# Seven-product groups in a decoder trunk: four products add up in one PSUM bank, and the last is put off into the next group

## The chip, the cores and the metric

The kernel runs on one core of a Trainium2 chip. A core has five engines with instruction queues of their own: TensorE (PE in the profile; its weight loads are listed apart as PEld), VectorE (DVE), ScalarE (ACT), GpSimd (POOL) and SyncE (SP, which here issues most of the weight transfers). Matmul results land in PSUM, eight banks of 128 partitions by 512 fp32 numbers; operands lie in SBUF. Each engine works through its queue in order and waits on semaphores where it needs another's result.

The metric is the time of one execution on the device in microseconds, as a median of several runs; lower is better.

## The reference

A two-layer decoder trunk on 512 tokens of width 1024, in float32: layer 0 mixes tokens by gated linear attention (GLA), layer 1 by stick-breaking attention (SB), and each layer is wrapped by two half-step feed-forward blocks (FFN), so there are four FFNs:

```python
x = x + 0.5 * swiglu(rmsnorm(x, ffn1_norm[i]), ffn1_w_gate[i], ffn1_w_up[i], ffn1_w_down[i])
h = rmsnorm(x, mix_norm[i])
y = gla_mixer(h, ...) if i % 2 == 0 else sb_mixer(h, ...)
x = x + y
x = x + 0.5 * swiglu(rmsnorm(x, ffn2_norm[i]), ffn2_w_gate[i], ffn2_w_up[i], ffn2_w_down[i])
# swiglu(h, g, u, d) = (silu(h @ g) * (h @ u)) @ d, with 1024 x 2816, 1024 x 2816 and 2816 x 1024 weights
```

A final rmsnorm ends it. The change lies in the four FFNs alone.

## The kernel before, in words

Activations are kept transposed: eight tiles `xs[k]` of 128 features by 512 tokens. Every fp32 product is made of three matmuls of rounded parts: an operand is cut into a high part (a cast on ACT) and a low part (a subtraction on DVE), and high·high, low·high and high·low are added up in PSUM (`mm3`; in the seven-product groups the loop in `prod`, L540 to L547). The cuts of the weights are lines 135 (ACT) and 136 (DVE), those of the activations lines 631 and 632.

**Feed.** The work of all phases that eats weights is one list of entries, `feed.q`. Starting an entry cuts the weights of the next entries and issues the transfers of the ones behind (`Feed.start`), then runs the entry's body, which issues its matmuls and evacuations.

**An FFN** works through eleven chunks of 256 columns of the gate and up weights, gathered in the groups of `GROUPS`, (0,2), (2,4), (4,6), (6,8), (8,9), (9,11). After a group, the matching rows of the down weights are multiplied with its hidden tiles `hs` in `down` entries, which are interleaved with the chunks of the next group. A `down` of a four-tile group takes 24 matmuls of 512 columns in two PSUM tiles; one of the two-tile group (8,9) 24 in four PSUM tiles. The last group's `down` entries stand at the end of the FFN (in the last FFN `back_tok` instead, behind transposes in `to_tokens`).

**Seven-product groups.** A dense chunk (1024 x 256 weights, 512 tokens) is cut into 2 x 2 x 2 blocks, eight products of 512 x 128 weights by 256 tokens. For the gate of chunks 3 to 10 and the up of chunks 2 to 10, `seven` replaces them by seven products and some additions (a Strassen-Winograd scheme). That makes 17 such groups in each FFN, 68 in all. Each product is 12 matmuls of 256 columns (four blocks of the contraction, three each). Two feed entries make a group: `body_1` with products 1 to 4 and `body_2` with 5 to 7. Before the change:

- product 1 goes to bank `w` and is copied out to `u2` (ACT, L580); product 2 goes to `z` and DVE adds it to `u2` (L556);
- product 3 goes to `q` and is copied to `c5` (ACT, L587); product 4 adds to product 1 in `w`, which is then the first half of the left result tile `o0` (`left`, L560 or L562);
- product 5 goes to the second half of the bank of `z` (called `y`); DVE adds `u2` to it (`u3`, L556), and then `c5` (L600), which is the second half of `o1`;
- product 6 adds to product 3 in `q`, DVE adds `u2` (L556), and `rest` finishes `o0` (L566 for a gate, L569 for an up);
- product 7 goes to the second half of the bank of `w`, DVE adds `u3` (L556), and `rest` finishes `o1`.

For a gate group `left` and `rest` are a Silu on ACT, and the tiles go to `self.gates`. For an up group they multiply with a gate tile on DVE, and `close` cuts the product into `hh` and `hl` and appends it to `hs`.

**Order.** Outside a few stretches marked as scheduled by hand, a planner in the framework lays out each engine's queue. It runs the program through a model of the engines' times and issues, among what is ready in that model, the instruction that stands first in the program. A tile whose slot is still held makes its instructions not ready. It also puts in every semaphore wait. Two accesses of one PSUM bank by different engines are kept apart by a wait even where they touch different columns.

**Banks.** `psum(name)` without a tag deals banks in the fixed round `order = "aazzztto"` over four pools of 2, 3, 2 and 1 banks. A seven-product group takes three turns, a `feat` one, a `down` two or four.

Of the kernel before, what the change touches and what calls it, by code (L numbers as in the profile page):

```python
# [19 lines left out]
P = 128  # L20
# [12 lines left out]
def decoder(ctx: ExitStack, tc: tile.TileContext, a: dict, out: bass.AP):  # L33
# [257 lines left out]

                feed.q.append(Entry([u], body))

    def down(w, r0, nf, hs, part, nxt):

        nd = KD // nf
        src = w[r0 : r0 + nf * P, part * nd * P : (part + 1) * nd * P]
        ch = Chunk(src.rearrange("(f p) c -> p f c", p=P), nf, nd * P)
        ch.few = True

        def body(W):
            (wh, wl), = W
            for m in range(nd):
                ps = psum("ps_d")
                s = slice(m * P, (m + 1) * P)
                for f in range(nf):
                    mm3(ps, wh[:, f, s], wl[:, f, s], hs[f][0], hs[f][1], f == 0, f == nf - 1)
                k = part * nd + m
                x = like(xs[k], 4)
                nc.vector.scalar_tensor_tensor(  # L310
                    out=x, in0=back_by(ps, 4), scalar=0.5, in1=x, op0=ALU.mult, op1=ALU.add
                )
                if nxt is not None:
                    nxt(k)
                yield

        feed.q.append(Entry([(ch, lambda t: t, nf, nd * P)], body))
# [135 lines left out]
    class FFN:  # L453
# [10 lines left out]
        def __init__(self, wg, wu, wd, gi, nxt, first=False, last=False):  # L464
            self.gi, self.normed, self.first = gi, False, first
            self.evac_g_, self.evac_u_ = self.evac_g, lambda ps: self.evac_u(ps, 0)
            if first:
                self.NORMED = 8
            self.defer, self.gates = [], []
            self.lead = []  # L470
            self.hs = [[] for _ in self.GROUPS]
            base, downs = len(feed.q), []
            self.base = base
            self.sums_by = 10**6
            for group, (c0, c1) in enumerate(self.GROUPS):
                slots, put = 2 * (c1 - c0), 0
                for i in range(slots):
                    c, f = c0 + i // 2, i % 2
                    if f == 0:
                        g, u = Chunk(cols(wg, c * 256, 256), KD, 256), Chunk(cols(wu, c * 256, 256), KD, 256)  # L480
                    d = self.defer if i == 0 and c == 0 else None
                    f_ = f
                    if first and c == 0:

                        g, u = (Chunk(cols(w, f * P, P), KD, P) for w in (wg, wu))
                        self.lead += [g, u]
                        f_ = 0
                    if c >= self.SEVEN:
                        if f == 0:
                            self.seven(g)  # L490
                    elif c not in self.SEVEN_UP:
                        feat(g, f_, self.evac_g, defer=self.defer if first and i == 1 else d, o=quads, m=four)
                    elif f == 0:
                        feat(g, 0, self.evac_g, o=quads, m=four), feat(g, 1, self.evac_g, o=quads, m=four)
                    if c not in self.SEVEN_UP:
                        feat(u, f_, lambda ps, h=group: self.evac_u(ps, h), defer=d, o=quads, m=four)
                    elif f == 1:
                        while c < self.SEVEN and put < len(downs) // 2:
                            down(*downs[put])
                            put += 1  # L500
                        self.sums_by = min(self.sums_by, len(feed.q) - base)
                        self.seven(u, group)

                    while c >= self.SEVEN and put < len(downs) * (i + 1) // slots:
                        down(*downs[put])
                        put += 1
                for x in downs[put:]:
                    down(*x)
                n = 2 * (c1 - c0)
                end = group + 1 == len(self.GROUPS)  # L510
                downs = [(wd, c0 * 256, n, self.hs[group], part, nxt if end else None) for part in range(n)]
            self.count = len(feed.q) - base
            if last:
                back_tok(wd, c0 * 256, n, self.hs[group], nxt)
            else:
                for x in downs:
                    down(*x)
            self.total = len(feed.q) - base

        def seven(self, ch, group=None):  # L520
# [31 lines left out]
            def part(name):  # L552
                return self.tp.tile([P, H], F32, tag="c", bufs=2, name=name)
# [10 lines left out]
            def rest(o, c):  # L564
# [4 lines left out]
                nc.vector.tensor_tensor(out=o[:, c:T], in0=o[:, c:T], in1=self.gates.pop(0)[:, c:T], op=ALU.mult)  # L569
                self.close(o, group)  # L570

            def body_1(W):
                ax, s = W

                v["w"], v["z"], v["q"] = psum("ps_w"), psum("ps_z"), psum("ps_q")
                w, z, q = (v[n][:, 0:H] for n in "wzq")
                v["o"] = self.tp.tile([P, T], F32, tag="t", name="o0")
                prod(w, ax, 0, half(0, 0))
                v["u2"] = part("u2")
                nc.scalar.copy(v["u2"], w)  # L580
                yield
                prod(z, s, 4, lambda j: self.t_half(1, j))
                add(v["u2"], z, v["u2"])
                yield
                prod(q, s, 0, lambda j: self.t_half(0, j))
                v["c5"] = part("c5")
                nc.scalar.copy(v["c5"], q)  # L587
                yield
                prod(w, ax, 4, half(4, 0), first=False)
                left(v["o"], w)  # L590
                yield

            def body_2(W):
                s, a22 = W
                q, y = v["q"][:, 0:H], v["z"][:, H:T]
                o0, o1 = v["o"], self.tp.tile([P, T], F32, tag="t", name="o1")
                prod(y, s, 0, lambda j: self.t_half(2, j))
                u3 = o1[:, 0:H]
                add(u3, y, v["u2"])
                nc.vector.tensor_tensor(out=o1[:, H:T], in0=u3, in1=v["c5"], op=ALU.add)  # L600
                yield
                prod(q, s, 4, half(4, 1), first=False)
                add(o0[:, H:T], q, v["u2"])
                rest(o0, H)
                yield
                o = v["w"][:, H:T]
                prod(o, a22, 0, lambda j: self.t_half(3, j))
                add(o1[:, 0:H], o, u3)
                rest(o1, 0)
                yield  # L610


            feed.q.append(Entry([(ch, lambda t: t[:, :, 0:P], KD, P), (ch, sums_12, KD, P)], body_1))
            feed.q.append(Entry([(ch, sums_34, KD, P), (ch, lambda t: t[:, 4:8, P:], 4, P)], body_2))

        def t_half(self, i, j):

# [71 lines left out]
        def run(self, between=None):  # L689
            with tc.tile_pool(name="hp", bufs=8, reuse_waits="tile") as self.hp, tc.tile_pool(  # L690
                name="tp", bufs=5, reuse_waits="tile"
            ) as self.tp:
                st["few"] = self.hp
                new_norm()

                if self.first:
                    with tc.manual_schedule():
                        feed.entries(1)
                        stats_b(turned=True)
                        flush(self.defer)  # L700
                else:
                    two_halves(stats_a)
                    stats_b(turned=True)
                    flush(self.defer)
                done = feed.pos - self.base
                for job, n in ((self.normed_input, self.NORMED - done), (self.sums, self.sums_by - self.NORMED)):
                    todo = list(job())
                    for i in range(n):
                        for piece in todo[i * len(todo) // n : (i + 1) * len(todo) // n]:
                            piece()  # L710
                        feed.entries(1)
                    self.normed = True
                    st["h"], st["l"] = zip(*self.n)
                feed.entries(self.count - self.sums_by)
                if between is not None:
                    with tc.issue_after(st["silu"]):
                        nc.scalar.preload_act_table_set("sqrt_and_others")
                    feed.q[feed.pos].split()
                    between(self.tp)
                feed.entries(self.total - self.count)  # L720
# [844 lines left out]
```

## Time and profile before

| what | value |
|---|---|
| median of 3 runs | 1797.32 us (1796.83 to 1797.62) |
| the profiled execution | 1798.32 us |
| its span, first to last instruction | 1796.5 us |
| mean granted TensorE clock | 0.997 |
| PE busy | 1771.0 us, 12,502 matmuls |
| DVE busy | 1450.4 us |
| ACT busy | 906.9 us |
| GLA mixer, about | 345 to 600 us |
| SB mixer, about | 1220 to 1460 us |

A busy share counts the time from an instruction's start to its end. Matmuls overlap in the array, so the profile's mean of one matmul is longer than the distance from one start to the next. How densely PE works is read from starts: in the chain that ended last, a run of matmuls is given with its start, its length and its count.

### The profile page before, as it was taken

What the parts mean: (1) busy time and instruction counts of PE and PEld (TensorE: products, weight loads), DVE (VectorE), ACT (ScalarE), POOL (GpSimd) and SP (SyncE); (2) the same over time, 40 slices, a digit from 0 to 9 for tenths busy, and PEclk for the clock granted to TensorE, in tenths of its full rate; (3) what the DMA queues carried; (4) which work ended last, traced back from release to release, by engine and by line L of the source; (5) the groups of instructions that cost most, each with busy time, mean ns of one, the idle gap of its engine ahead of it and who ended that gap; (6) DMA issues with size and microseconds to landing.
All of it is one profiled execution on the core that took longest, in us unless ns stands there. A gap on an engine that the chain in (4) does not pass through costs nothing.

```text
span 1796.5 us, 30288 instructions
## 1 busy us (share of the span) xinstructions
PE 1771.0 (99%) x12502; PEld 1622.2 (90%) x12502; DVE 1450.4 (81%) x2371; ACT 906.9 (50%) x1428; POOL 9.6 (1%) x23
## 2 busy tenths in 40 slices
PE   9999999999999999999999999999999999999998
PEld 7899999888988899999989999998877888999997
DVE  7988887787868988878898888786777579888785
ACT  6544445455645444444554444454777544544444
POOL 0000000100000000000000000000000000000000
PEclk9999999999999999999999999999999999999999
DMA  6243333321222333333333333322222223333321
GB/s 212 71 133 114 106 118 103 96 72 57 87 71 94 117 106 106 106 113 100 107 111 101 106 106 118 106 83 83 59 71 71 71 94 118 106 106 111 125 83 71
DMA packets 177614, 179.19 MB, mean 100 GB/s; under 512 B 4098, under 2 KB 167988, under 8 KB 177476
## 3 DMA queue, kind: packets, MB, share of 16 engines
q1 hardware_dynamic: 176224, 175.13, 30.4%
q8 instruction: 98, 1.61, 0.4%
q0 software_dynamic: 576, 1.05, 0.2%
q10 hardware_dynamic: 676, 1.07, 0.2%
q14 instruction: 40, 0.33, 0.1%
HBM read 175.17 MB, written 2.10 MB: 99 GB/s over the span
## 4 chain that ended last, share of the span: by engine, by line
PE 84%; DVE 9%; ACT 3%; DMA 3%; issue 1%; SPq 0%; DVEq 0%; ACTq 0%
PE ps_d L64 24%; PE ps_w L545 15%; PE ps_f L64 13%; PE ps_z L545 10%; PE ps_q L545 10%; PE ps_t L64 4%; PE ps_b L64 4%; DVE wl L136 2%; DMA raw<-in_ffn_w_up_dram 2%; DVE l L1211 1%; PE ps_bt L64 1%; ACT wh L135 1%; PE ps_z L1167 1%; DVE r L1219 1%; DMA raw<-in_sb_w_in_dram 1%
## 5 line engine op out<-in xcount | busy, mean ns | idle before, releaser
L136 DVE TENSOR_TENSOR wl<-raw,wh 128x1024 fp32r<-128x1024 f32 x242 | 259.4, 1073 | 72.2 <-ACT wh L135 71.6
L135 ACT CAST wh<-raw 128x1024 fp32r<-128x1024 f32 (+1 forms) x242 | 223.9, 927 | 149.4 <-PE ps_f L64 53.1
L64 PE MATMUL ps_d<-hh,wh 128*128 128x512 f32 x672 | 254.9, 379 | 0.0
L64 PE MATMUL ps_d<-hh,wl 128*128 128x512 f32 x672 | 254.7, 379 | 0.0
L64 PE MATMUL ps_d<-hl,wh 128*128 128x512 f32 x672 | 254.7, 379 | 0.0
L135 ACT CAST wh<-s 128x1024 fp32r<-128x1024 f32 x136 | 142.2, 1046 | 117.0 <-PE ps_q L545 80.3
L136 DVE TENSOR_TENSOR wl<-s,wh 128x1024 fp32r<-128x1024 f32 x136 | 166.0, 1222 | 24.1 <-ACT wh L135 23.0
L64 PE MATMUL ps_f<-xh,wh 128*128 128x512 f32 x464 | 180.7, 390 | 0.3 <-DVE ol L1257 0.2
L64 PE MATMUL ps_f<-xh,wl 128*128 128x512 f32 x464 | 176.9, 381 | 0.5 <-DVE wl L1444 0.4
L64 PE MATMUL ps_f<-xl,wh 128*128 128x512 f32 x464 | 177.0, 381 | 0.0
L310 DVE SCALAR_TENSOR_TENSOR x<-ps_d,x 128x512 f32<-128x512 f32 x184 | 125.2, 689 | 60.9 <-PE ps_d L64 60.7
L545 PE MATMUL ps_z<-th,wh 128*128 128x256 f32 x544 | 150.1, 276 | 0.2 <-DVE u L556 0.2
L545 PE MATMUL ps_w<-nh,wl 128*128 128x256 f32 x544 | 149.6, 275 | 0.0
L545 PE MATMUL ps_w<-nl,wh 128*128 128x256 f32 x544 | 149.6, 275 | 0.0
L545 PE MATMUL ps_z<-th,wl 128*128 128x256 f32 x544 | 149.6, 275 | 0.0
L545 PE MATMUL ps_z<-tl,wh 128*128 128x256 f32 x544 | 149.6, 275 | 0.0
L545 PE MATMUL ps_w<-nh,wh 128*128 128x256 f32 x544 | 149.5, 275 | 0.0
L135 ACT CAST wh<-rawd 128x1024 fp32r<-128x1024 f32 x84 | 88.0, 1048 | 121.5 <-PE ps_d L64 103.2
L64 PEld LDWEIGHTS ps_d<-hl,wh 128*128 128x128 f32 x672 | 127.0, 189 | 18.0
L64 PEld LDWEIGHTS ps_d<-hh,wl 128*128 128x128 f32 x672 | 127.2, 189 | 16.5
L64 PEld LDWEIGHTS ps_d<-hh,wh 128*128 128x128 f32 x672 | 127.2, 189 | 16.5
L136 DVE TENSOR_TENSOR wl<-rawd,wh 128x1024 fp32r<-128x1024 f32 x84 | 102.8, 1224 | 34.5 <-ACT wh L135 34.1
(279 smaller groups left out, 4621.6 us busy)
## 6 DMA issues: line engine op xcount, KB each, us to landing
raw<-in_ffn_w_gate_dram SPq DMA_DIRECT2D x43, 1024.0 KB, 5.2
raw<-in_ffn_w_up_dram SPq DMA_DIRECT2D x43, 1024.0 KB, 5.2
rawd<-in_ffn_w_down_dram SPq DMA_DIRECT2D x84, 512.0 KB, 3.4
raw<-in_gla_w_in_dram SPq DMA_DIRECT2D x12, 1024.0 KB, 5.1
raw<-in_sb_w_in_dram SPq DMA_DIRECT2D x16, 512.0 KB, 3.8
raw<-in_gla_w_out_dram SPq DMA_DIRECT2D x4, 1024.0 KB, 5.0
raw<-in_sb_w_in_dram SPq DMA_DIRECT2D x4, 1024.0 KB, 5.2
raw<-in_sb_w_out_dram SPq DMA_DIRECT2D x4, 1024.0 KB, 4.9
```

Source lines behind the costliest of these rows:

```text
L64: st["pe"] = nc.tensor.matmul(ps, l, r, start=first, stop=last).ins
L135: nc.scalar.copy(h, r).ins,
L136: nc.vector.tensor_tensor(out=l, in0=r, in1=h.bitcast(F32), op=ALU.subtract).ins,
L310: nc.vector.scalar_tensor_tensor(out=x, in0=back_by(ps, 4), scalar=0.5, in1=x, op0=ALU.mult, op1=ALU.add)
L545: nc.tensor.matmul(pairs(o), l_, r_, start=first and j + n == 0, stop=j == 3 and n == 2, skip_group_check=True)
L1167: nc.tensor.matmul(o, l, r, start=first, stop=False, skip_group_check=True)
L1211: nc.vector.tensor_tensor_scan(out=l[:, c][:, ::-1], data0=r[:, c][:, ::-1], data1=l[:, c][:, ::-1], initial=0.0, op0=ALU.add, op1=ALU.add,)
L1219: nc.vector.tensor_tensor(out=r, in0=ps[:, 0:w], in1=l, op=ALU.subtract)
```

## The change

The group keeps its seven products and their operands, and their order and the places where they are added up change. Product 1 is copied by ACT from `w` into the bank of `z` in PSUM. Product 2 is added there by PE itself (`first=False`), and the sum is copied out to `u2` by ACT. Product 5 is added by PE onto the same bank, and DVE adds `c5` to it on the way out into the second half of `o1`. Product 7 is added onto the same bank too, and `left` and `rest` finish `o1` from there. Product 7 and what follows it are not issued in `body_2` but kept in `self.later` and issued by `put_off`: in the next group's `body_1` behind product 3, ahead of a `down` whose hidden tiles are not complete, or at the end of the FFN's groups in `run`. The order within a group is now 1, 3, (7 of the group before), 2, 4, 6, 5. The second halves of the banks `w` and `z` are no longer used.

```diff
-    def down(w, r0, nf, hs, part, nxt):
+    def down(put_off, w, r0, nf, hs, part, nxt):
...
             (wh, wl), = W
+            if len(hs) < nf:
+                put_off()
             for m in range(nd):
...
-            self.lead = []
+            self.lead, self.later = [], []
...
                 prod(w, ax, 0, half(0, 0))
-                v["u2"] = part("u2")
-                nc.scalar.copy(v["u2"], w)
-                yield
-                prod(z, s, 4, lambda j: self.t_half(1, j))
-                add(v["u2"], z, v["u2"])
+                nc.scalar.copy(z, w)
                 yield
                 prod(q, s, 0, lambda j: self.t_half(0, j))
                 v["c5"] = part("c5")
                 nc.scalar.copy(v["c5"], q)
                 yield
+                self.put_off()
+                prod(z, s, 4, lambda j: self.t_half(1, j), first=False)
+                v["u2"] = part("u2")
+                nc.scalar.copy(v["u2"], z)
+                yield
                 prod(w, ax, 4, half(4, 0), first=False)
                 left(v["o"], w)
...
-                prod(y, s, 0, lambda j: self.t_half(2, j))
-                u3 = o1[:, 0:H]
-                add(u3, y, v["u2"])
-                nc.vector.tensor_tensor(out=o1[:, H:T], in0=u3, in1=v["c5"], op=ALU.add)
-                yield
                 prod(q, s, 4, half(4, 1), first=False)
                 add(o0[:, H:T], q, v["u2"])
                 rest(o0, H)
                 yield
-                o = v["w"][:, H:T]
-                prod(o, a22, 0, lambda j: self.t_half(3, j))
-                add(o1[:, 0:H], o, u3)
-                rest(o1, 0)
+                prod(z, s, 0, lambda j: self.t_half(2, j), first=False)
+                o1 = self.tp.tile([P, T], F32, tag="t", name="o1")
+                add(o1[:, H:T], z, v["c5"])
                 yield
 
+                def fourth():
+                    prod(z, a22, 0, lambda j: self.t_half(3, j), first=False)
+                    left(o1, z)
+                    rest(o1, H)
+
+                self.later.append(fourth)
...
+        def put_off(self):
+            while self.later:
+                self.later.pop()()
...
                 feed.entries(self.count - self.sums_by)
+                self.put_off()
                 if between is not None:
```

More of the change, by code (lines that the diff above doesn't have):

```diff
@@ L510, in __init__ @@
                 end = group + 1 == len(self.GROUPS)
-                downs = [(wd, c0 * 256, n, self.hs[group], part, nxt if end else None) for part in range(n)]
+                downs = [(self.put_off, wd, c0 * 256, n, self.hs[group], part, nxt if end else None) for part in range(n)]
             self.count = len(feed.q) - base
@@ L573, in body_1 @@
                 ax, s = W
-                v["w"], v["z"], v["q"] = psum("ps_w"), psum("ps_z"), psum("ps_q")
-                w, z, q = (v[n][:, 0:H] for n in "wzq")
+                v["w"], v["z"], v["q"] = (psum(n)[:, 0:H] for n in ("ps_w", "ps_z", "ps_q"))
+                w, z, q = (v[n] for n in "wzq")
                 v["o"] = self.tp.tile([P, T], F32, tag="t", name="o0")
                 prod(w, ax, 0, half(0, 0))
-                v["u2"] = part("u2")
-                nc.scalar.copy(v["u2"], w)
-                yield
-                prod(z, s, 4, lambda j: self.t_half(1, j))
-                add(v["u2"], z, v["u2"])
+                nc.scalar.copy(z, w)
                 yield
@@ L594, in body_2 @@
                 s, a22 = W
-                q, y = v["q"][:, 0:H], v["z"][:, H:T]
-                o0, o1 = v["o"], self.tp.tile([P, T], F32, tag="t", name="o1")
-                prod(y, s, 0, lambda j: self.t_half(2, j))
-                u3 = o1[:, 0:H]
-                add(u3, y, v["u2"])
-                nc.vector.tensor_tensor(out=o1[:, H:T], in0=u3, in1=v["c5"], op=ALU.add)
-                yield
+                q, z = v["q"], v["z"]
+                o0 = v["o"]
                 prod(q, s, 4, half(4, 1), first=False)
```

## The prediction, made before the changed kernel was run

> **What bounds the kernel now.** I read the page's busy times first:
>
> ```profile
> span 1796.5 us, 30288 instructions
> ...
> PE 1771.0 (99%) x12502; PEld 1622.2 (90%) x12502; DVE 1450.4 (81%) x2371; ACT 906.9 (50%) x1428; POOL 9.6 (1%) x23
> ```
>
> PE is busy nearly throughout, and DVE is second at 81%. A busy PE need not be a dense one, since matmuls overlap. So I read next the chain that ended last, in order of time, at the end of the first FFN (start, length, what, count):
>
> ```profile
> 303.83 2.68 PE ps_w L545 x24
> 306.51 1.34 PE ps_z L545 x12
> 307.85 1.34 PE ps_q L545 x12
> 309.19 1.34 PE ps_w L545 x12
> 310.53 1.34 PE ps_z L545 x12
> 311.87 1.34 PE ps_q L545 x12
> 313.21 1.34 PE ps_w L545 x12
> 314.55 25.90 PE ps_d L64 x120
> 340.45 10.36 PE ps_f L64 x48
> ```
>
> One whole group (the second half of the first row to the start of `ps_d`) takes 7 x 1.34 = 9.38 us for 84 matmuls, 0.1117 us from start to start. The `down` matmuls stand 25.90 / 120 = 0.2158 us apart. Nothing but PE is in this chain. Whether that holds for a long stretch is seen by counting the matmuls of 200 us of the FFN, those of line 545 (256 columns) and those of line 64 (512 columns) apart:
>
> ```profile
> 100.00:300.00 200.00, 128.38 (x1132) 128.45 (x1133) 1.00 0.34 111
> ...
> 100.00:300.00 200.00, 75.71 (x342) 63.32 (x340) 1.00 0.34 111
> ```
>
> 1132 x 0.1117 + 342 x 0.2158 = 126.4 + 73.8 = 200.2 us. The stretch is full: PE starts a matmul at every possible moment, at a granted clock of 1.00. The third view is who PE waited for in line 545, and the stretches in which PE does stand:
>
> ```profile
>   DVE u L556: 0.6, 2
> ...
> 345.00:600.00 255.00, 248.72 (x2236) 220.22 (x2236) 199.22 (x406) 134.50 (x222) 0.00 (x0) 0.99 0.25 78
> ...
> 1250.00:1450.00 200.00, 192.78 (x1258) 160.90 (x1259) 142.15 (x211) 143.58 (x287) 0.00 (x0) 1.00 0.21 67
> ```
>
> Over all 68 seven-product groups PE and its weight loads waited 0.6 us, at two places, for DVE's addition to `u2`. Of the 25.5 us without a matmul (1796.5 - 1771.0), 6.3 lie in the GLA mixer and 7.2 in the SB mixer. The rest lies mostly at the two ends of the kernel. So the FFNs, which the change touches, are bound by the number of matmuls, and the stages with slack are others.
>
> **The change part by part.** The matmuls: seven products of 12 before, seven of 12 after, the same widths and operands. 0 us, unless PE begins to wait.
>
> What leaves and joins DVE and ACT is costed from these groups (line, operation, operands, count, busy time and mean in ns, idle time before):
>
> ```profile
> L556 DVE TENSOR_TENSOR u<-ps_z,u 128x256 f32<-128x256 f32 x68 | 28.6, 421 | 10.1 <-PE ps_z L545 10.0
> L556 DVE TENSOR_TENSOR o<-ps_z,u 128x256 f32<-128x256 f32 x68 | 28.5, 419 | 0.0
> L556 DVE TENSOR_TENSOR o<-ps_w,o 128x256 f32<-128x256 f32 x68 | 28.6, 421 | 0.0
> L569 DVE TENSOR_TENSOR o<-o,o 128x512 f32<-128x512 f32 x32 | 22.1, 690 | 0.0
> L562 DVE TENSOR_TENSOR o<-ps_w,o 128x256 f32<-128x256 f32 x32 | 13.4, 418 | 0.0
> L580 ACT COPY u<-ps_w 128x256 f32<-128x256 f32 x68 | 25.4, 374 | 20.3 <-PE ps_w L545 19.8
> L566 ACT ACTIVATE o<-o 128x512 f32<-128x512 f32 x32 | 20.2, 632 | 19.0 <-DVE o L556 19.0
> L560 ACT ACTIVATE o<-ps_w 128x256 f32<-128x256 f32 x32 | 12.3, 384 | 0.1
> ```
>
> DVE loses the first three, 68 each: 85.7 us. In the 36 up groups its one multiplication of 512 (0.69 us) becomes two of 256 (0.42 each): 36 x 0.15 = 5 us back. ACT gets 68 more copies of 256 at 0.374: 25 us (one of them writes PSUM, which no row here shows; I take the copy that writes SBUF). In the 32 gate groups the Silu of 512 (0.632) becomes two of 256 (2 x 0.384): 4 us more. So DVE falls to some 1370 us busy and ACT rises to some 936. None of this moves the end: in the FFNs the cover for both is a PE that is full. Were that cover gone, the 80 us of DVE would be the prize. No transfer and no queue order on SP or POOL is touched.
>
> (a) The wait that goes. Product 5 no longer shares a bank with an addition on DVE: -0.6 us.
>
> (b) The new waits on ACT's copies. Product 2 now needs the copy of `w` into `z`, product 5 the copy of `z` into `u2`. Behind a waiting product stands the whole of PE's queue. Two products lie between, or 2.68 us, and in the first group of an FFN, with nothing put off yet, one, or 1.34. The copies take 0.37 and start promptly: they idled before for 19.8 us over 68 waiting for PE, so ACT stands ready. What can be ahead of them in the queue is a cast of the weights on ACT (on DVE, for (c), a cut), and the handover from PE's last start to a waiting engine is read from the timeline of PE and DVE:
>
> ```profile
> L135 ACT CAST wh<-s 128x1024 fp32r<-128x1024 f32 x136 | 142.2, 1046 | 117.0 <-PE ps_q L545 80.3
> L136 DVE TENSOR_TENSOR wl<-s,wh 128x1024 fp32r<-128x1024 f32 x136 | 166.0, 1222 | 24.1 <-ACT wh L135 23.0
> ...
> 314.28 0.28 PE L545 MATMUL ps_w<-tl,wh 128*128 128x256 f32 x1
> ...
> 314.59 0.42 DVE L556 TENSOR_TENSOR o<-ps_w,o 128x256 f32<-128x256 f32 x1
> ```
>
> 0.37 + 1.05 plus the handover of 314.59 - 314.28 = 0.3 is 1.7, below 2.68 and 0.4 above 1.34. Bounds 0 to 4 x 0.4 = 1.6 us; I take 0, the promptness being the nearer row.
>
> (c) Held banks. `z` is now held until product 7 in the next group. By the code's round of eight turns, the next `q` is six turns on where one `down` of two tiles lies between, but eight where four tiles do (around chunks 8 to 10). Following the round through the pools, that bank is really the same at two groups of each FFN, eight in all. There product 3 must wait until `left` has read product 7. The planner can issue product 7 and then product 2 (1.34 us) meanwhile. `left` takes 0.42 on DVE, behind a cut of 1.22 at worst: 0.3 + 1.22 + 0.42 - 1.34 = 0.6. Bounds 0 to 8 x 0.6 = 4.8; I take 0.05 each, 0.4, because the next operation on DVE or ACT is more often short or waiting than a cut just begun.
>
> (d) The tails. At the end of three FFNs product 7 is now followed at once by the `down` entries that need its `hl`; before, a `down` of another group (24 x 0.2158 = 5.2 us) lay between. (In the last FFN, 32 transposes lie between.) The first three hidden tiles give 9 matmuls, and `hl` is read two later: 11 x 0.2158 = 2.4 us of cover. The way from product 7 to `hl` before, in the timelines of DVE and ACT at the same place:
>
> ```profile
> 315.96 0.68 DVE L569 TENSOR_TENSOR o<-o,o 128x512 f32<-128x512 f32 x1
> ...
> 317.16 1.22 DVE L136 TENSOR_TENSOR wl<-rawd,wh 128x1024 fp32r<-128x1024 f32 x1
> 318.29 0.69 DVE L632 TENSOR_TENSOR hl<-o,hh 128x512 fp32r<-128x512 f32 x1
> ...
> 316.68 0.62 ACT L631 CAST hh<-o 128x512 fp32r<-128x512 f32 x1
> ```
>
> From PE's last start at 314.28 to the end of the low part at 318.29 + 0.69 = 318.98: 4.7 us, of which the operations alone, as the change has them, are 0.3 + 0.42 + 0.42 + 0.62 + 0.69 = 2.5. So each tail stands between 0.1 and 4.7 - 2.4 = 2.3 us, if PE keeps to the program's order. The planner need not keep to it: it fills a hole that it foresees with matmuls from behind. That it does so is seen in the chain after the FFN:
>
> ```profile
> 364.54 2.64 PE ps_z L64 x6
> 367.18 2.79 PE ps_f L64 x12
> 369.97 0.66 PE ps_z L64 x2
> ```
>
> The eight `ps_z` matmuls (four gate tiles, two each) stand together in the program; twelve of a later projection were put between. At a tail the next output tile's first nine matmuls could be drawn forward in the same way, 1.9 us. Bounds 0 to 3 x 2.3 = 6.9; I take 0.3 each, 0.9, nearer the lower end because of that filling.
>
> Sum: -0.6 + 0 + 0.4 + 0.9 = +0.7 us on the profiled execution: 1798.32 + 0.7 = 1799.0, of which 1796.5 + 0.7 is span. That execution lies 1.0 above the median of the runs, so I predict 1798.0.
>
> **The rivals.**
>
> Faster, by DVE's freed 80 us: the planner could bring forward the mixers' opening work on DVE, so that PE stands less there. For it: DVE was 81% busy, and the casts and cuts stand in the chain in the opening of GLA. Against it: DVE's relief is over before the mixers' own chains begin, and their waits (6.3 + 7.2 us of PE) are of work that cannot start in the FFN. A third of these: -4.5, 1797.3 - 4.5 = 1792.8. Chance 0.10.
>
> Slower, by the tails: the planner does not foresee the hole, and product 7's way to `hl` is as long as before. 3 x 2.3 - 0.6 = +6.3: 1803.6. It decides once a tail stands over 1.4 us (3 x 1.4 - 0.6 = 3.6). For it: DVE's updates of `x` and a cut are queued at that place. Against it: the filling just shown, and that DVE has five additions less ahead. Chance 0.14.
>
> The change does not do what it says: at the eight places of (c) the planner must issue product 7 early, and puts it straight behind product 5. It then waits for DVE's addition of `c5`: 0.3 + 0.42 + 0.4 for the handover back, or 1.1 us, and up to 1.2 more behind a cut. 8 x 1.1 - 0.6 = +8: 1805. Against it: at that moment a `down` is ready, and it stands first in the program. Chance 0.06.
>
> The clock: where PE stands often enough, the granted clock falls. The only stretch that shows it is the end of the kernel, besides the start:
>
> ```profile
> 1760.00:1797.00 37.00, 29.04 (x151) 26.22 (x149) 21.42 (x46) 15.58 (x35) 0.00 (x0) 0.95 0.15 58
> ```
>
> There 8 us without a matmul go with 5% less clock, 1.9 us of 37. At each of the 11 places of (c) and (d), that would be 11 x 1.9 = 20 us: 1818. Against it: with 6.3 us of standing in the GLA mixer the clock was still 0.99. Chance 0.03. The Trainium skill speaks of this case ("TensorE: Matmul & The Clock Gate", section "A second HAM failure mode: psum-queue depth-cycling"): a kernel that cycled through PSUM banks let PE idle briefly between groups, often enough that its clock kept falling back. By that rule the new dependences on one bank would cost the 1818; by the row of the GLA mixer, hardly anything.
>
> **How the numbers follow.** The forecast has 0.67, the rivals 0.10, 0.14, 0.06 and 0.03. A change of under 0.2% (3.6 us) can't be told from none. The forecast's own range is 1796 to 1801: of its 0.67 I put 0.01 below 1793.7 and 0.03 above 1800.9. So faster 0.10 + 0.01 = 0.11, slower 0.14 + 0.06 + 0.03 + 0.03 = 0.26, the same 0.63. The range for 8 in 10 goes from 1793.5, most of the way to the first rival, to 1804.5, past the tails' 1803.6 and (b) with (c) at half.
>
> **What would show it.** Right: still 84 starts in 9.38 us per group, PE waits in line 545 under 1 us, DVE busy near 1370 and ACT near 936, with the time unchanged. Step (b) wrong: PE or weight loads of `ps_z` waiting for an ACT copy. (c) wrong: `ps_q` waiting for `left`. (d) wrong: `ps_d` waiting for L632 or L631 at some 318, 1200 and the end of the second FFN. The forecast falls if the matmuls' distance in the groups changes though nothing waits, or if the mixers' stretches change by over 3 us.

## The result, and the profile after

The changed kernel takes 1953.81 us (median of 4, 1949.27 to 1955.38) beside 1797.47 us before (median of 4, 1796.83 to 1799.82). The ratio is 1.0863, 95% interval 1.0843 to 1.0884. It is 8.6% slower, where I forecast no change and put the range's upper end at 1804.5.

The first view is the busy times of the changed kernel's page, with the row of the granted clock in 40 slices and the chain that ended last by engine:

```profile
span 1951.7 us, 30166 instructions
...
PE 1818.6 (93%) x12502; PEld 1652.9 (85%) x12502; DVE 1387.1 (71%) x2203; ACT 1098.0 (56%) x1654; POOL 9.6 (0%) x23
...
PEclk9999999999989999999999999997888799999999
...
PE 69%; ACT 17%; DVE 9%; DMA 3%; issue 1%; SPq 0%; ACTq 0%; DVEq 0%
```

DVE fell to 1387, near the 1370 that the sum had. ACT rose to 1098 instead of 936, and its share of the chain went from 3% to 17%. Late in the span the clock is down to 0.7 and 0.8. To place the loss I cut both kernels at the first seven-product matmul of each FFN, so that a stretch holds the FFN's groups and what follows them. First the kernel before, then the changed one:

```profile
76.90:628.40 551.50, 545.23 (x4297) 499.58 (x4296) 451.50 (x787) 272.52 (x420) 7.81 (x15) 0.99 0.30 97
628.40:956.30 327.90, 327.67 (x2213) 306.44 (x2213) 275.14 (x433) 151.98 (x218) 0.00 (x0) 1.00 0.33 107
956.30:1522.30 566.00, 558.30 (x3709) 501.54 (x3709) 442.82 (x692) 312.34 (x524) 0.54 (x1) 1.00 0.29 92
```

```profile
77.30:653.80 576.50, 550.16 (x4297) 501.53 (x4296) 435.08 (x745) 319.55 (x477) 7.81 (x15) 0.99 0.29 93
653.80:982.40 328.60, 328.12 (x2213) 306.27 (x2213) 258.20 (x392) 157.59 (x243) 0.00 (x0) 1.00 0.33 106
982.40:1675.90 693.50, 599.49 (x3709) 530.22 (x3709) 430.57 (x650) 443.11 (x641) 0.54 (x1) 0.93 0.24 75
```

The columns are the window, its length, the busy times (and counts) of PE, PEld, DVE, ACT and POOL, the granted clock, the DMA share and GB/s. The middle stretch, from FFN to FFN with no mixer between, grew by 0.7 us. The one with the GLA mixer grew by 25.0 and the one with the SB mixer by 127.5. Both mixers are code that the change does not touch. In the SB stretch PE stands 86.3 us more (693.50 - 599.49 against 566.00 - 558.30), and its busy time is 41.2 us longer for the same 3709 matmuls, at a clock of 0.93. Next, the group of ACT on line 452 that is new, and PE's longest waits for ACT (total, times, longest):

```profile
L452 ACT ACT_TABLE_LOAD x122 | 156.5, 1283 | 4.4 <-DVE vv L1025 2.2
```

```profile
PE ps_T L1242 <- ACT wt L452: 73.1, 16, 7.0
PE ps_oT L1257 <- ACT wt L452: 8.3, 5, 2.5
```

ACT evaluates exponentials, logarithms and Silu from tables, and a load brings a set of them in. Before, the whole kernel made 6 loads; now it makes 132, and 122 of them stand in the mixers, in front of `act`, the helper for their exponentials and logarithms. That is 156.5 us on ACT, on the mixers' way from the logits to the weights that PE waits for. What set them off stands at the end of the first FFN, in ACT's timeline. Before:

```profile
307.19 0.63 ACT L566 ACTIVATE o<-o 128x512 f32<-128x512 f32 x1 [0.27 <-DVE o L556]
307.84 1.28 ACT L445 ACT_TABLE_LOAD   x1
```

After:

```profile
305.74 0.72 ACT L568 ACTIVATE o<-o 128x256 f32<-128x256 f32 x2
306.37 0.36 ACT L583 COPY ps_z<-ps_w 128x256 f32<-128x256 f32 x1
306.75 1.28 ACT L447 ACT_TABLE_LOAD   x1
...
309.45 1.28 ACT L562 ACT_TABLE_LOAD   x1
310.74 0.39 ACT L562 ACTIVATE o<-ps_z 128x256 f32<-128x256 f32 x1
```

The code behind line 447 (445 before) is outside the diff:

```python
def exp_ln_tables(after):            # a mixer calls it with st["silu"]
    with tc.issue_after(after):
        st["tab"] = nc.scalar.preload_act_table_set("natural_log_exp_and_others").ins
def act(o, i, fn, **kw):             # the mixers' Exp and Ln
    with tc.issue_after(st["tab"]): ...
```

`st["silu"]` is the Silu that `rest` traced last, and the set for both functions is loaded behind it. Before, that was one Silu of 512 over the whole of `o1`, and no other came after it. The change splits it: `left` does the left half when product 7 is done, `rest` the right half, whose input is ready at product 5. In the program `left` stands first; in the planner's order it comes second, because it waits for the put-off product. So the pair at 305.74 holds the right half's Silu, the common set is loaded at 306.75, and at 309.45 a set for Silu is loaded over it. The mixers then start without the common set. From there each switch between an exponential and a logarithm has a load in front of it, as in the SB mixer:

```profile
1350.09 0.60 ACT L452 ACTIVATE wt<-ps_T 128x512 f32<-128x512 f32 x1
1350.70 1.28 ACT L452 ACT_TABLE_LOAD   x1
1352.00 0.63 ACT L452 ACTIVATE l<-l 128x512 f32<-128x512 f32 x1
...
1353.62 1.28 ACT L452 ACT_TABLE_LOAD   x1
1354.91 0.63 ACT L452 ACTIVATE l<-l 128x512 f32<-128x512 f32 x1
```

### The profile page after: what moved, and what is told of

It is laid out like the page before. It is cut to its first block, busy times and chain, and to the rows that moved or that the text cites. A ratio compares the mean times of both kernels' runs of the same rounds, so it can differ in the third digit from the quotient of the medians.

```text
span 1951.7 us, 30166 instructions
## 1 busy us (share of the span) xinstructions
PE 1818.6 (93%) x12502; PEld 1652.9 (85%) x12502; DVE 1387.1 (71%) x2203; ACT 1098.0 (56%) x1654; POOL 9.6 (0%) x23
## 4 chain that ended last, share of the span: by engine, by line
PE 69%; ACT 17%; DVE 9%; DMA 3%; issue 1%; SPq 0%; ACTq 0%; DVEq 0%
PE ps_d L64 20%; PE ps_z L547 12%; PE ps_f L64 11%; PE ps_q L547 9%; PE ps_w L547 8%; ACT L452 7%; PE ps_b L64 3%; DVE wl L136 3%; ACT l L452 3%; ACT wh L135 2%; DMA raw<-in_ffn_w_up_dram 1%; PE ps_t L64 1%; ACT l L1211 1%; PE ps_bt L64 1%; PE ps_z L1177 1%
## 5 line engine op out<-in xcount | busy, mean ns | idle before, releaser
L136 DVE TENSOR_TENSOR wl<-raw,wh 128x1024 fp32r<-128x1024 f32 (+1 forms) x242 | 259.4, 1072 | 189.4 <-ACT wh L135 188.9
L547 PE MATMUL ps_z<-tl,wh 128*128 128x256 f32 x816 | 224.5, 275 | 0.0
L547 PE MATMUL ps_z<-th,wl 128*128 128x256 f32 x816 | 224.5, 275 | 0.0
L547 PE MATMUL ps_z<-th,wh 128*128 128x256 f32 x816 | 224.4, 275 | 0.0
L64 PE MATMUL ps_f<-xh,wh 128*128 128x512 f32 x464 | 188.4, 406 | 0.1
L64 PE MATMUL ps_f<-xh,wl 128*128 128x512 f32 x464 | 183.5, 395 | 0.6 <-DVE wl L1454 0.4
L64 PE MATMUL ps_f<-xl,wh 128*128 128x512 f32 x464 | 182.4, 393 | 0.0
L452 ACT ACT_TABLE_LOAD x122 | 156.5, 1283 | 4.4 <-DVE vv L1025 2.2
L547 PEld LDWEIGHTS ps_z<-th,wh 128*128 128x128 f32 x816 | 156.7, 192 | 0.1
L547 PEld LDWEIGHTS ps_z<-th,wl 128*128 128x128 f32 x816 | 156.7, 192 | 0.1
L547 PEld LDWEIGHTS ps_z<-tl,wh 128*128 128x128 f32 x816 | 156.7, 192 | 0.0
```

The source lines that it names most:

```text
L64: st["pe"] = nc.tensor.matmul(ps, l, r, start=first, stop=last).ins
L136: nc.vector.tensor_tensor(out=l, in0=r, in1=h.bitcast(F32), op=ALU.subtract).ins,
L452: st["last"] = nc.scalar.activation(o, i, fn, **kw).ins
L547: nc.tensor.matmul(pairs(o), l_, r_, start=first and j + n == 0, stop=j == 3 and n == 2, skip_group_check=True)
```

## The experiments

Three theories stood against each other. T: the loads of tables, set off by the order of two Silus, are the whole loss, and the groups themselves cost next to nothing. W: PE's new waits on the shared bank and the put-off products cost it. C: the clock falls because PE idles in the groups.

**Silus in order.** The changed kernel with an order on ACT between the two halves of a gate tile:

```diff
-                    nc.scalar.activation(o[:, 0:H], w, AF.Silu)
+                    st["left"] = nc.scalar.activation(o[:, 0:H], w, AF.Silu).ins
...
                     left(o1, z)
-                    rest(o1, H)
+                    if group is None:
+                        with tc.issue_after(st["left"]):
+                            rest(o1, H)
+                    else:
+                        rest(o1, H)
```

> The changed kernel, with one thing added: in a gate group the Silu of the right half of o1 (rest) is queued on ACT behind the Silu of the left half (left), so that the mixers' activation table is loaded behind both. Nothing else differs. Theory T (the table): the changed kernel's 132 table loads become 6 as before, the mixers take as long as before, and what stays is the seven-product groups' own cost, read from the FFN between the GLA and the SB mixer as +0.7 us per pass: about 1797.5 + 4 x 0.7 = 1800 us, 1797 to 1804. Rival W (PE's new waits on the shared bank and the put-off products): those stay as they are, so the time stays above 1900. Rival C (the clock falls because PE idles in the groups): stays above 1900 too.

Measured: 1803.61 us beside 1800.38 of the kernel before on the same chip, ratio 1.0020 (1.0009 to 1.0030), and 6 table loads. ACT's timeline at the same place has both halves ahead of the load:

```profile
308.12 0.38 ACT L562 ACTIVATE o<-ps_z 128x256 f32<-128x256 f32 x1
308.39 0.41 ACT L568 ACTIVATE o<-o 128x256 f32<-128x256 f32 x1
308.82 1.28 ACT L447 ACT_TABLE_LOAD   x1
```

T holds; W and C fall as causes of the 8.6%. What stays of the change is +0.2%, and PE's waits show where some of it lies:

```profile
PE ps_d L64 <- ACT hh L644: 3.0, 2, 1.9
...
PE ps_q L547 <- DVE o L564: 1.5, 4, 0.4
```

The first is the tails of step (d), the second the held banks of step (c).

**The loss without the change.** The kernel before, with `st["silu"]` taken from a Silu that is not the last:

```diff
-                    st["silu"] = nc.scalar.activation(o[:, c:T], o[:, c:T], AF.Silu).ins
+                    ins = nc.scalar.activation(o[:, c:T], o[:, c:T], AF.Silu).ins
+                    if c:
+                        st["silu"] = ins
```

> The kernel before, with its own products and banks, and one edit: the Silu behind which the mixers' activation table is queued is the last one of a left tile o0, not that of o1, which comes after it. So one Silu falls behind the load. T: the table loads go from 6 to about 132 without any of the change's products, and the time goes to about 1797 + 155 = 1950 us (1930 to 1970). W and C: the products, banks and waits are those of before, so about 1797.

Measured: 1952.12 us, ratio 1.0847 (1.0817 to 1.0876). The groups of table loads on ACT are the changed kernel's, count for count:

```profile
L450 ACT ACT_TABLE_LOAD x122 | 156.5, 1283 | 4.4 <-DVE vv L1017 2.2
L566 ACT ACT_TABLE_LOAD x3 | 3.8, 1283 | 0.1
```

One edit to the place of a table load makes the loss with the old products, banks and waits. The new groups are not needed for it.

**One mixer mended.** As the kernel with Silus in order, with the order kept in the first FFN alone (`if group is None and self.first`).

> The changed kernel, with the order of the two Silus kept in the first FFN alone, so that only the GLA mixer gets its table loaded for good; the SB mixer and the end stay as in the changed kernel. T: 100 table loads; the GLA mixer gives back the 25 us that it grew by (576.5 - 551.5 us from the first seven-product matmul of the first FFN to that of the second), so about 1954 - 25 = 1929 us, 1922 to 1936. W and C: no change, 1954.

Measured: 1928.42 us, ratio 1.0715 (1.0691 to 1.0739), with 100 table loads. The two stretches with mixers:

```profile
76.90:628.70 551.80, 543.85 (x4297) 498.06 (x4297) 434.12 (x745) 278.40 (x445) 7.83 (x15) 1.00 0.31 97
...
957.30:1650.40 693.10, 602.79 (x3709) 532.18 (x3708) 430.98 (x650) 443.26 (x641) 0.54 (x1) 0.92 0.24 75
```

The GLA stretch is back at 551.8 from 576.5, the SB stretch stays at 693.1. So the loss goes with the loads mixer by mixer: the 32 loads that went (132 to 100) are worth 24.7 us, 0.8 us each; the 91 of SB 127 us, 1.4 us each, the slower matmuls included. A load alone is 1.283.

**The same disorder, with a second load.** The changed kernel as it is, and another load of the common set behind the late Silu:

```diff
-            st["tab"] = nc.scalar.preload_act_table_set("natural_log_exp_and_others").ins
+            nc.scalar.preload_act_table_set("natural_log_exp_and_others")
+        with tc.issue_after(st["left"]):
+            st["tab"] = nc.scalar.preload_act_table_set("natural_log_exp_and_others").ins
```

> The changed kernel, its Silus out of order as they are, with a second load of the mixers' table queued behind the late Silu of the left half. It leaves the extra loads around that Silu (12 table loads in all) and takes away only that the mixers run with no common table. T: if the price of the change is the mixers' loads between exponentials and logarithms, 110 of the 132 loads go and the time is that of the first run plus at most 4 x 1.3 us: 1800 to 1809. If it is the Silus' order itself, or anything in the groups, 1954.

Measured: 1803.69 us, ratio 1.0019 (1.0009 to 1.0030), 12 loads, so 120 of the 132 went. The Silus' order costs nothing in itself that shows beside the 1.0020 with Silus in order, nor do six more loads outside the mixers. What costs is that the mixers lack the common set.

**What putting off is worth.** The kernel with Silus in order, with product 7 in its own group, right behind product 5 (`fourth()` in place of `self.later.append(fourth)`).

> The kernel of the first run (Silus in order), with product 7 issued in its own group behind product 5 instead of being put off. The four additions in one bank stay. It tells the price of the waits that putting off is there to avoid. If the wait for DVE's addition of c5 (0.3 + 0.42 us and a handover, up to 1.2 more behind a cut) falls on PE in each of the 68 groups: 68 x 1.0 = 68, about 1870 us. If the planner fills it with matmuls from the entries behind, the time is that of the first run, 1797 to 1804. I expect something between, nearer the first: 1800 to 1850.

Measured: 1834.14 us, ratio 1.0189 (1.0171 to 1.0207). PE now waits for the addition of `c5`:

```profile
PE ps_z L547 <- DVE o L558: 17.0, 42, 2.0
```

Putting product 7 off is worth some 30 us, half of the 68 that a full wait in each group would make. The listed waits are only 17.0 us, but PE's busy time grew too, by 19.2 us for the same 12,502 matmuls at the same mean clock (1791.6 against 1772.4), so the list understates the standing.

**Product 7 in the middle of a `down`.** The kernel with Silus in order, with

```diff
-            if len(hs) < nf:
-                put_off()
             for m in range(nd):
+                if m == nd // 2 or len(hs) < nf:
+                    put_off()
```

> The kernel of the first run (Silus in order), with product 7 issued earlier where a down entry lies between: in the middle of that entry instead of in the next group. So the shared bank is given back before the round of eight turns comes to it again, and at the end of an FFN half a down entry (12 matmuls, 2.6 us) lies between product 7 and the entries that need it. If what is left of the change's cost (+3.6 us in the first run) is the held bank (PE waits of 0.54 us per FFN at ps_q) and the tails (PE waits for the cut of o1, 2.05 and 1.30 us), it goes: 1797 to 1800 us beside a kernel before of the same chip of about 1800, a ratio of 0.998 to 1.001. If it is something else in the new groups, the ratio stays at 1.002.

Measured: 1813.84 us, ratio 1.0072 (1.0059 to 1.0085): a miss, slower instead of faster. The waits of (c) and (d) are gone from PE's list, and another takes their place:

```profile
PE ps_z L547 <- DVE o L558: 6.6, 11, 1.4
```

Half a `down`, 2.6 us, is too little at these 11 places for DVE's addition of `c5`, which stands behind cuts of 1.22 us in DVE's queue. DVE's timeline at the longest of them, and the matmul that waits:

```profile
1070.75 1.22 DVE L136 TENSOR_TENSOR wl<-raw,wh 128x1024 fp32r<-128x1024 f32 x1
1071.88 1.22 DVE L136 TENSOR_TENSOR wl<-s,wh 128x1024 fp32r<-128x1024 f32 x1
...
1073.36 0.41 DVE L558 TENSOR_TENSOR o<-ps_z,c 128x256 f32<-128x256 f32 x1
...
1073.82 0.38 PE L547 MATMUL ps_z<-th,wh 128*128 128x256 f32 x1 [1.40 <-DVE o L558]
```

Counting the `ps_d` matmuls ahead of them, ten of the 11 lie before the `down` entries of chunks 6 and 7, where the kernel with Silus in order lists no wait of PE. So the next version moves it at fewer places, and farther.

**Product 7 late in a `down`, at few places.** The kernel with Silus in order, with

```diff
-            if len(hs) < nf:
-                put_off()
+            second = r0 == 6 * 2 * P and part % 2 == 1
             for m in range(nd):
+                if len(hs) < nf or (m == 0 and second) or (m == 3 and nd == 4):
+                    put_off()
```

> The kernel of the first run (Silus in order), with product 7 issued earlier only at the places where it is held too long or needed too soon: around chunk 8 behind one whole down entry (5.2 us) ahead of the second, and behind three quarters of the entries of four tiles (3.9 us) around chunks 9 and 10 and at the end of an FFN. Everywhere else it stays in the next group. If what is left of the change is the held banks and the tails, and half a down entry was only too little time for DVE's addition of c5, the PE waits at ps_q (0.54 us per FFN), at ps_d for the cut of o1 and at ps_z for the addition (6.6 us in the fifth kernel) are all under 1 us in sum, and the ratio is 0.999 to 1.001. If three quarters are too little too, 1.001 to 1.004. If the change's groups cost something that is no wait at these places, 1.002 as in the first run.

Measured: 1796.78 us beside 1800.34, ratio 0.9986 (0.9977 to 0.9995), just below the forecast's 0.999. No wait of the groups' `ps_z` and `ps_q` or of `ps_d` is left in PE's list. Two things differ from the version before, the places and the distance. Ten of its 11 waits were at places that are not moved here, so that 3.9 to 5.2 us is enough where 2.6 was not isn't shown. The stretches:

```profile
76.70:626.20 549.50, 543.36 (x4298) 497.73 (x4298) 433.88 (x745) 278.02 (x445) 7.82 (x15) 1.00 0.31 97
626.20:953.50 327.30, 327.30 (x2214) 306.28 (x2213) 258.24 (x392) 157.48 (x243) 0.00 (x0) 1.00 0.34 107
953.50:1519.90 566.40, 558.42 (x3709) 501.52 (x3708) 424.42 (x648) 317.87 (x549) 0.54 (x1) 1.00 0.30 92
```

This is the one version faster than both kernels, by 0.14% of the kernel before. That this small lead comes from the change is not shown: in the profile 1.9 of the 2.0 us gained in the GLA stretch are PE's busy time (543.36 against 545.23), at a granted clock of 1.00 against 0.99. The pure FFN stretch is 0.6 us shorter than before. By the prediction's distances its 1429 matmuls of 256 columns and 785 of 512 take 1429 x 0.1117 + 785 x 0.2158 = 329.0 us, no less than its 327.30, so there is no more to be had there from waits.

**What DVE's time is worth.** The kernel before, with the addition of line 600 done four times (the same result each time).

> The kernel before, with the addition of c5 (L600) done four times over, to the same result: 204 more DVE operations of 0.42 us, 86 us, on the way that the change would relieve by as much. It asks what DVE's time is worth in the FFNs. If PE is the cover, as the prediction has it: 1797 to 1803, ratio under 1.003. If DVE, at 81%, already bears on the end: up to 86 us more, 1820 to 1885.

Measured: 1809.48 us, ratio 1.0046 (1.0031 to 1.0061), between the two forecasts. The additions are 0.41 us long, but in a row they start 0.33 apart (87.08, 87.41 and 87.75, another operation in the middle), and DVE's busy time grew by 58.7 us (1509.1 against 1450.4), not by 86. It cost 8 to 9 us: about a seventh comes through, and PE's list shows where a part of it lies (the kernel before had 0.2, 1 in this row):

```profile
PE ps_z L545 <- DVE u L556: 3.5, 6, 1.2
```

PE is the cover that the prediction took it for, but not a whole one. An operation added to DVE makes the additions that PE needs soon later, now and then too late.

## Why the prediction was wrong, point by point

**The bound, right.** The FFNs are bound by the count of matmuls. The pure FFN stretch moved by 0.7 us when its products were rearranged and 17 us of its DVE time left (328.60 against 327.90; DVE 258.20 against 275.14). In the kernel with Silus in order (the kernel in order, below) DVE's busy time fell by 69 us, where 81 was forecast.

**The step that failed** is the sentence on ACT: "In the 32 gate groups the Silu of 512 (0.632) becomes two of 256 (2 x 0.384): 4 us more", and "None of this moves the end" behind it. As a duration it was right. In the kernel that runs in order, ACT has 929 us busy, where 936 was forecast. But the Silu that was split is the one that `st["silu"]` names, and the table load of the following mixer is queued behind it and it alone. With two halves the planner chose their order by readiness, and the right half, ready two products sooner, went first. I wrote that no queue order on SP or POOL is touched and did not ask the same of ACT. The rows to see it in were there: ACT's timeline of before has line 566 and the table load back to back, and its whole execution has 6 loads. The step was worth some 150 us of the 155 by which the span grew (1951.7 against 1802.1 with Silus in order), in place of 0; the GLA stretch grew by 25.0 and the SB stretch by 127.5.

The Trainium skill has the rule for this in "ScalarE: Activation LUTs", section "Table sets: the hidden batching unit": calls should be batched by set, and a logarithm followed by an exponential takes one load, since one set holds both. Here that held only where the common set was loaded by hand behind every Silu. The section "What ACT_TABLE_LOAD costs" gives 1283 ns for a load, which the trace agrees with (1283), and some 1380 ns of draining beside it for each switch. By an estimate from that section's figures, 126 extra loads would take 126 x 2.66 = 335 us of ACT; the span grew by 155. No draining shows in the rows of the SB mixer above: the load starts at 1350.70, as the activation before it ends (1350.09 + 0.60), and the next activation follows 1.30 us after the load's start.

**(a)** was right: the wait for the addition to `u2` is gone. **(b)** was right: PE waits for no copy into or out of `z` (lines 583 and 592) in the changed kernel.

**(c)** had the right mechanism, and a size that was too small. I took 0.4 us in sum. In the kernel in order PE waits at `ps_q` once in each FFN (1.5 us listed over the 4), and the matmul starts 0.54 us late there: 4 x 0.54 = 2.2. PE waits at one place in each FFN, where I counted two.

**(d)** had the right place, and a cover that was too long. I took 0.9 of bounds of 0 to 6.9; the kernel in order waits 3.0 us for `hh` at two tails. I counted eleven matmuls up to the use of `hl`, and leaned on the planner's filling. PE's timeline of the kernel in order at the first tail, the last two rows of ten `ps_d` matmuls:

```profile
321.00 0.38 PE L64 MATMUL ps_d<-hl,wh 128*128 128x512 f32 x1
323.27 0.48 PE L64 MATMUL ps_d<-hh,wh 128*128 128x512 f32 x1 [1.89 <-ACT hh L644]
```

Nine matmuls of the `down` run on the three hidden tiles that are ready (319.27 to 321.38), and then PE stands for 1.89 us until `hh` of the last tile is there, two matmuls ahead of `hl`. They are the first output tile's own nine; none of the next tile's was put into the hole. DVE's timeline shows what `left` of product 7 (L564) stands behind, updates of `x` and a cut, as the rival of the tails had it:

```profile
319.82 1.28 DVE L312 SCALAR_TENSOR_TENSOR x<-ps_d,x 128x512 f32<-128x512 f32 x2
321.02 1.21 DVE L136 TENSOR_TENSOR wl<-rawd,wh 128x1024 fp32r<-128x1024 f32 x1
322.15 0.41 DVE L564 TENSOR_TENSOR o<-ps_z,o 128x256 f32<-128x256 f32 x1
```

**The sum** without the tables, +0.7, stands beside a measured +0.2% (0.09 to 0.30%), or 1.6 to 5.4 us; (c) and (d) at their measured 2.2 and 3.0 with (a) at -0.6 give +4.6. Taking the bounds' lower parts was wrong by about 4 us, too little to leave the range.

**The rivals.** Faster by DVE's relief: not seen (in the kernel in order the GLA stretch is 550.9 against 551.5 and the SB stretch 571.0 against 566.0). The tails: real, at half their price. That product 7 falls behind product 5: not seen; the kernel that does it costs 1.9%. The clock: its cause was not the bank. It did fall, to 0.93 in the SB stretch, through up to 7.0 us of waiting for ACT at a time. Of the 127.5 us there, 86.3 are standing and 41.2 are slower matmuls; both went when the loads went.

The prediction's reading of the clock was wrong in one point. It took the end of the kernel for the only stretch with a lower clock, besides the start. Shorter windows of the kernel before show two more, in the GLA mixer, which a mean of 0.99 over 255 us hid:

```profile
430.00:435.00 5.00, 4.74 (x43) 4.71 (x44) 3.73 (x16) 0.63 (x1) 0.00 (x0) 0.66 0.01 3
510.00:515.00 5.00, 5.00 (x17) 4.07 (x16) 3.04 (x11) 1.08 (x2) 0.00 (x0) 0.69 0.00 0
```

Each is worth about 1.6 us, by an estimate from these rows (5 x 0.34 and 5 x 0.31). The first follows a standing of 1.91 us that ends at 430.26; but after the 1.89 us at the tail above the clock stays at 1.00 (320 to 330), so a standing of this length does not decide it alone.

This accounts for most of another difference: the SB stretch of the kernel in order is 5.0 us longer than before. PE stands 1.4 us more there, about what the second tail and one held bank are listed with (1.1 and 0.4). Its busy time is 3.6 us longer (561.87 against 558.30) for the same 3709 matmuls. That profile has its two such spots in the SB mixer (1315 to 1325 at 0.84 and 0.82, 1400 to 1405 at 0.66) and none in the GLA mixer. Why they change places stays open.

## What to carry to other kernels

When an instruction is split, ask what else in the program hangs on it by name: a table load, a hook for order, a semaphore. Two halves with inputs of different age may change places under a planner that goes by readiness, and what was queued behind "the last" is then queued behind the wrong one. A count of table loads in the profile, set against the kernel before, shows this in one row. And a product put off needs a distance set by the queue of the engine it depends on, not just by the duration of the one operation: here 2.6 us was too short for an addition of 0.41 us behind two cuts.

## What the runs showed of the hardware

ACT takes 1.283 us for each table load (132 of them, all alike), and the loads of 91 switches in a chain from PE over ACT to PE cost 1.4 us each in time. They also brought the granted clock down, 0.93 over 693 us, though PE was busy 86% of that stretch; 41.2 of its 127.5 us are matmuls that took longer. I had not expected a clock that low from stalls of at most 7 us. Even in the kernel before, the clock was down for some 3.4 us in the GLA mixer: from 431.22 to 434.63 matmuls of 256 columns started 0.21 us apart instead of 0.11.
